# Loads, sums and stores of the output weights' blocks pinned to their written place

## The chip, the cores and the metric

The kernel runs on one core of one Trainium2 chip. The metric is the time of one execution in microseconds of the device (us). Below, PE is TensorE (matmuls), DVE is VectorE, ACT is ScalarE, POOL is GpSimd, and SP is SyncE, which here only issues DMAs; DMA is the set of 16 transfer engines that carry them out.

## The reference

One layer of a transformer trunk in float32 (sequence 1024, width 1024, 16 heads): a forgetting-attention mixer, then a SwiGLU channel mixer of width 2816, each between a modulation and a LayerNorm. The change lies in the channel mixer:

```
def swiglu(h, w_in, w_out):
    gate, up = jnp.split(h @ w_in, 2, axis=-1)
    return (jax.nn.silu(gate) * up) @ w_out

x = layer_norm(DEEPNORM_ALPHA * x + gate1 * y, ln_g[i, 0], ln_b[i, 0])
h = x * (1.0 + scale2) + shift2
x = layer_norm(DEEPNORM_ALPHA * x + gate2 * swiglu(h, ffn_w_in[i], ffn_w_out[i]), ln_g[i, 1], ln_b[i, 1])
```

## The kernel before

Every float32 product is made of three matmuls of a high and a low part (hi x hi, hi x lo, lo x hi). The kernel works in three long stages: attention (to about 720 us), the first product of the channel mixer ("first product", to about 1210 us) and the second product with the output weights ("second product", to the end). Both products of the channel mixer use a scheme with seven sub-products instead of eight (a Strassen form), so sums and differences of blocks are needed on both sides.

**First product.** `seq` is a list of 154 steps `(ff, i)`: ff is one of 22 column tiles of 128 hidden units, i the sub-product. The steps of ff 0 to 5 with i = 1 and 2 come first; then each ff from 0 to 5 has five steps (6, 7, 5, 4, 3), and from ff 6 on, at n = 42, each ff has seven (1, 6, 2, 7, 5, 4, 3). `step(n)` issues 12 matmuls of 512 columns (lines 1072 to 1074) into one of the banks A, B and D, and then what reads the bank: for i = 6, 7 and 4 DVE reads B (lines 1085, 1087, 1092), for i = 5 and 3 it reads D (lines 1089, 1096), for i = 1 and 2 ACT reads A (lines 1081, 1083). B and D have one buffer each, and a chain goes on adding in the same bank, so the matmuls of i = 7 have to wait until DVE has read the bank of i = 6, those of i = 4 until that of i = 7 is read, and those of i = 3 until that of i = 5. In the same step `prepare(n + 8)` splits the weights for a later step into high and low part: a cast on ACT (line 844) and a subtraction on DVE (line 845), which one of eight slots takes. ff and ff + 1 also share sums of hidden values (`hidden_sums`, lines 990 to 995, on DVE) that wait for POOL's products (line 1098) and are stored to DRAM (line 981, `sd`).

**The blocks of the output weights.** The second product needs differences of blocks of `ffn_w_out`. `out_weights(j, k)` makes them, for j = 0 to 10, in two 512 KB buffers that are free by then, `gate1b` and `gate2b`: at k = 0 it loads two blocks (line 1006, two DMAs of 512 KB on SP), at k = 7 DVE makes two differences (lines 1008 and 1009), at k = 8 two more (lines 1011 and 1012), and both buffers are stored to `td[j]` (line 1014, two DMAs of 512 KB). There is one set of buffers, so block j + 1 can be loaded when block j is stored. In the source `step(n)` calls it with

```
j, k = divmod(n - 7 * FIRST, 10)
if 0 <= j < NJ:
    out_weights(j, k)
```

so a block is written over ten steps: load at n = 42 + 10 j, differences seven and eight steps later, and the last store at n = 150 of 154.

**What sets the order.** Each engine runs its instructions in the order of its own list, and SP issues its DMAs likewise: an instruction that waits holds up all that stand behind it. The written order is not the order in the lists: before the program is built, a scheduler puts each engine's instructions in order by a simulation of its own of when each is ready, keeping only true dependences. `tc.keep_in_program_order(ins)` takes an instruction out of that freedom: it ties it behind the instruction that was written before it on the same engine. It adds no wait on another engine.

**Second product.** `prep2(m)` takes raw blocks `r` (a half from `sd`, a half from `ffn_w_out` or `td`, lines 870 to 875), casts them on ACT (line 1028) and subtracts on DVE (line 1029) into a ring of 14 places. `products` (lines 1221 to 1223) uses them. `done` (line 1180) copies the first sub-product's banks on ACT; the four banks lie in pairs in two tiles, y1_0 and y1_1.

Of the kernel before, what the change touches and what calls it, by code (L numbers as in the profile page):

```python
# [12 lines left out]
ALU = mybir.AluOpType  # L13
# [3 lines left out]
P = 128  # L17
# [28 lines left out]
def fox_trunk_kernel(  # L46
# [17 lines left out]
    nc = tc.nc  # L64
# [5 lines left out]
    fwo = ffn_w_out[0]  # L70
# [788 lines left out]
    td = [dram.tile([P, 2, 2, 512], F32, name=f"td{j}") for j in range(NJ)]  # L859
# [113 lines left out]
        return others  # L973

    banks, fds = {}, []

    def open_bank(tag, ff, n):
        banks[tag, ff] = psA.tile([P, 512], F32, name=f"{tag}{ff}", tag=tag, bufs=n)
# [21 lines left out]
    def out_weights(j, k):  # L1000

        b11, b12 = gate1b[:, 0:512], gate1b[:, 512:1024]
        b21, b22 = gate2b[:, 0:512], gate2b[:, 512:1024]
        if k == 0:
            for n, t in enumerate((gate1b, gate2b)):
                nc.sync.dma_start(t, fwo[(2 * j + n) * P:(2 * j + n + 1) * P, :])
        elif k == 7:
            nc.vector.tensor_tensor(b11, b12, b11, ALU.subtract)
            nc.vector.tensor_tensor(b12, b22, b12, ALU.subtract)
        elif k == 8:  # L1010
            nc.vector.tensor_tensor(b22, b22, b11, ALU.subtract)
            nc.vector.tensor_tensor(b21, b21, b22, ALU.subtract)
            for n, t in enumerate((gate1b, gate2b)):
                nc.sync.dma_start(td[j][:, n].rearrange("p c e -> p (c e)"), t)


    RING = 14
# [39 lines left out]
    def step(n):  # L1057
# [9 lines left out]
        if 0 <= j < NJ:  # L1067
            out_weights(j, k)
# [234 lines left out]
```

## Time and profile before

| what | value |
|---|---|
| median of 3 runs | 1439.01 us (1437.71 to 1443.9) |
| the profiled execution's own time | 1438.14 us |
| its span, first to last instruction | 1436.3 us |
| mean granted TensorE clock | 0.990 of full speed |
| PE busy | 1359.0 us, 95% |
| DVE, ACT, POOL busy | 1012.2, 584.2, 334.4 us |
| DMA moved | 254.41 MB, mean 177 GB/s |

The page gives busy time by engine over the whole span, and the span in 40 slices of 35.9 us. Busy shares are averages over stages with different limits: what a change in one stage is worth is read from that stage, in the tables by stretch, in the waits of PE there, and in the lists of instructions in order of time. In those lists the square bracket at a row's end is the engine's idle time before the instruction, and what ended it.

### The profile page before, as it was taken

What the parts mean: (1) busy time and instruction counts of PE and PEld (TensorE: products, weight loads), DVE (VectorE), ACT (ScalarE), POOL (GpSimd) and SP (SyncE); (2) the same over time, 40 slices, a digit from 0 to 9 for tenths busy, and PEclk for the clock granted to TensorE, in tenths of its full rate; (3) what the DMA queues carried; (4) which work ended last, traced back from release to release, by engine and by line L of the source; (5) the groups of instructions that cost most, each with busy time, mean ns of one, the idle gap of its engine ahead of it and who ended that gap; (6) DMA issues with size and microseconds to landing.
All of it is one profiled execution on the core that took longest, in us unless ns stands there. A gap on an engine that the chain in (4) does not pass through costs nothing.

```text
span 1436.3 us, 19137 instructions
## 1 busy us (share of the span) xinstructions
PE 1359.0 (95%) x6832; PEld 1134.0 (79%) x6832; DVE 1012.2 (70%) x1636; ACT 584.2 (41%) x1025; POOL 334.4 (23%) x250
## 2 busy tenths in 40 slices
PE   5899999999999999999999888999999999899997
PEld 4677778877888888879998667777788888788886
DVE  6866586555888888888778555767655556775897
ACT  3532232224777777774338222222223334533320
POOL 2442012210111111141000544434444431000011
PEclk9999999999999999999999999999999999999999
DMA  9757775558555555627463234777732336976531
GB/s 275 197 176 243 240 218 177 183 194 212 143 135 137 132 139 136 148 87 266 162 193 93 89 110 132 259 243 261 248 111 96 110 111 208 352 256 225 195 119 73
DMA packets 212305, 254.41 MB, mean 177 GB/s; under 512 B 13353, under 2 KB 138609, under 8 KB 212210
## 3 DMA queue, kind: packets, MB, share of 16 engines
q1 hardware_dynamic: 211058, 251.09, 57.9%
q10 hardware_dynamic: 1152, 2.10, 0.4%
q8 instruction: 54, 0.88, 0.3%
q14 instruction: 41, 0.34, 0.1%
HBM read 185.18 MB, written 67.96 MB: 176 GB/s over the span
## 4 chain that ended last, share of the span: by engine, by line
PE 63%; DVE 14%; DMA 9%; POOL 6%; issue 4%; ACT 2%; SPq 1%; POOLq 0%; DVEq 0%; ACTq 0%
PE og L631 5%; PE t L596 4%; PE y L1221 4%; PE y L1223 4%; PE y L1222 4%; PE B L1072 3%; PE B L1073 3%; PE B L1074 3%; PE s L535 2%; PE A L1072 2%; PE A L1074 2%; PE A L1073 2%; PE s L536 2%; PE o L579 2%; PE D L1074 2%
## 5 line engine op out<-in xcount | busy, mean ns | idle before, releaser
L1221 PE MATMUL y<-ring 128*128 128x512 f32 (+1 forms) x319 | 122.8, 385 | 4.7 <-ACT fpu L1180 4.3
L1072 PE MATMUL B<-XT,slots 128*128 128x512 f32 x264 | 106.9, 405 | 19.7 <-DVE fd L1085 16.7
L1029 DVE TENSOR_TENSOR ring<-r,ring 128x1024 fp32r<-128x1024 f32 x77 | 95.6, 1249 | 41.3 <-ACT ring L1028 36.2
L1028 ACT CAST ring<-r 128x1024 fp32r<-128x1024 f32 x77 | 80.5, 1053 | 107.7 <-PE y L1223 57.5
L1222 PE MATMUL y<-ring 128*128 128x512 f32 (+1 forms) x319 | 122.7, 385 | 0.0
L1223 PE MATMUL y<-ring 128*128 128x512 f32 (+1 forms) x319 | 122.4, 385 | 0.0
L602 DVE TENSOR_TENSOR pl<-t,ph 128x512 fp32r<-128x512 f32 x192 | 103.9, 549 | 14.8 <-ACT ph L601 13.4
L844 ACT CAST slots<-wi 128x512 fp32r<-128x512 f32 x88 | 54.2, 621 | 143.9 <-PE D L1073 73.0
L543 ACT ACTIVATE p<-s,nm 128x640 f32<-128x640 f32 (+7 forms) x128 | 95.5, 746 | 39.1 <-DVE nm L542 38.7
L601 ACT CAST ph<-t 128x512 fp32r<-128x512 f32 x192 | 90.9, 479 | 44.2 <-PE t L596 41.8
L1073 PE MATMUL B<-XT,slots 128*128 128x512 f32 x264 | 105.2, 399 | 0.0
L1074 PE MATMUL B<-XT,slots 128*128 128x512 f32 x264 | 105.0, 398 | 0.0
L542 DVE TENSOR_REDUCE nm<-s 128x1 f32<-128x640 f32 (+7 forms) x128 | 95.6, 748 | 2.5
L596 PE MATMUL t<-ident,p 128*128 128x128 f32 x576 | 95.7, 274 | 0.6 <-DVE pl L602 0.5
L596 PEld LDWEIGHTS t<-ident,p 128*128 128x128 f32 x576 | 71.3, 141 | 11.5 <-DVE pl L602 2.2
L1072 PEld LDWEIGHTS B<-XT,slots 128*128 128x128 f32 x264 | 50.9, 193 | 36.1 <-DVE fd L1085 21.8
L579 PE MATMUL o<-ph,va 128*128 128x512 f32 x192 | 76.6, 399 | 0.0
L845 DVE TENSOR_TENSOR slots<-wi,slots 128x512 fp32r<-128x512 f32 x88 | 71.0, 807 | 7.7 <-ACT slots L844 7.7
L1221 PEld LDWEIGHTS y<-ring 128*128 128x128 f32 x319 | 60.3, 189 | 18.1 <-ACT fpu L1180 4.7
L535 PE MATMUL s<-ka,qa 128*128 128x320 f32 (+2 forms) x192 | 67.5, 352 | 4.8 <-ACT p L543 4.8
L1223 PEld LDWEIGHTS y<-ring 128*128 128x128 f32 x319 | 60.4, 189 | 11.8
L1072 PE MATMUL A<-h2h,slots 128*128 128x512 f32 x176 | 69.2, 393 | 0.6 <-ACT fc L1081 0.6
(571 smaller groups left out, 3731.8 us busy)
## 6 DMA issues: line engine op xcount, KB each, us to landing
wi<-in_ffn_w_in_dram SPq DMA_DIRECT2D x50, 512.0 KB
aw<-in_ada_w_dram SPq DMA_DIRECT2D x46, 512.0 KB
r<-sd SPq DMA_DIRECT2D x77, 256.0 KB
sd<-hs SPq DMA_DIRECT2D x44, 256.0 KB
r<-td SPq DMA_DIRECT2D x44, 256.0 KB
sd<-fd SPq DMA_DIRECT2D x33, 256.0 KB
r<-in_ffn_w_out_dram SPq DMA_DIRECT2D x33, 256.0 KB
qa<-qs SPq DMA_DIRECT2D x32, 256.0 KB
```

The lines of the kernel that those rows point to most:

```text
L535: nc.tensor.matmul(o, qa[:, q], ka[:, c0:c0 + w], start=True, stop=False)
L542: nc.vector.tensor_reduce(nm, view, axis=axis, op=ALU.max, negate=True)
L579: nc.tensor.matmul(o[:, c0:], va[:, kbk, :], ph[:, c0:], start=(kbk == 0), stop=False)
L596: nc.tensor.transpose(tb[:, jj * P:(jj + 1) * P], probs[hf * 4 + jj][:, kbk * P:(kbk + 1) * P], ident)
L602: nc.vector.tensor_tensor(pl[:, c0:], tb[:, c0:], f32(ph[:, c0:]), ALU.subtract)
L1029: nc.vector.tensor_tensor(t[:, 1], raw, f32(t[:, 0]), ALU.subtract)
L1072: nc.tensor.matmul(b, hi, rh, start=(first and k == 0), stop=False, skip_group_check=True)
L1073: nc.tensor.matmul(b, hi, rl, start=False, stop=False, skip_group_check=True)
L1074: nc.tensor.matmul(b, lo, rh, start=False, stop=(k == 3), skip_group_check=True)
L1221: nc.tensor.matmul(b[:, c0:c1], sh, wh, start=first, stop=False, skip_group_check=True)
L1222: nc.tensor.matmul(b[:, c0:c1], sh, wl, start=False, stop=False, skip_group_check=True)
L1223: nc.tensor.matmul(b[:, c0:c1], sl, wh, start=False, stop=last, skip_group_check=True)
```

## The change

Each instruction that `out_weights` issues (per block two loads, four differences on DVE and two stores) is passed to `keep_in_program_order`. Nothing else is edited. One line is added above them, so a line number above 976 is one higher in the changed kernel.

```
     banks, fds = {}, []
+    keep = tc.keep_in_program_order
...
         if k == 0:
             for n, t in enumerate((gate1b, gate2b)):
-                nc.sync.dma_start(t, fwo[(2 * j + n) * P:(2 * j + n + 1) * P, :])
+                keep(nc.sync.dma_start(t, fwo[(2 * j + n) * P:(2 * j + n + 1) * P, :]))
         elif k == 7:
-            nc.vector.tensor_tensor(b11, b12, b11, ALU.subtract)
-            nc.vector.tensor_tensor(b12, b22, b12, ALU.subtract)
+            keep(nc.vector.tensor_tensor(b11, b12, b11, ALU.subtract))
+            keep(nc.vector.tensor_tensor(b12, b22, b12, ALU.subtract))
         elif k == 8:
-            nc.vector.tensor_tensor(b22, b22, b11, ALU.subtract)
-            nc.vector.tensor_tensor(b21, b21, b22, ALU.subtract)
+            keep(nc.vector.tensor_tensor(b22, b22, b11, ALU.subtract))
+            keep(nc.vector.tensor_tensor(b21, b21, b22, ALU.subtract))
             for n, t in enumerate((gate1b, gate2b)):
-                nc.sync.dma_start(td[j][:, n].rearrange("p c e -> p (c e)"), t)
+                keep(nc.sync.dma_start(td[j][:, n].rearrange("p c e -> p (c e)"), t))
```

The order of instructions differs in three places that the prediction speaks of. The first is DVE's list where ff 6 ends and ff 7 begins. B and D are the banks (B6 is B of ff 6), `slots` the split weights, `fd` the hidden values, `hs` their sums. Before:

```order
L1087 TENSOR_TENSOR fd_8631<-B6_9209,fc_8277 128x512
L845 TENSOR_TENSOR slots_7830<-sqb_8409,slots_7830 128x512
L1008 TENSOR_TENSOR gate1b_106<-gate1b_106 128x512
L1089 TENSOR_TENSOR fd_8631<-D6_9268,fd_8631 128x512
L845 TENSOR_TENSOR slots_7830<-wi71_22_9042,slots_7830 128x512
L1009 TENSOR_TENSOR gate1b_106<-gate2b_107,gate1b_106 128x512
L1011 TENSOR_TENSOR gate2b_107<-gate2b_107,gate1b_106 128x512
L1092 TENSOR_TENSOR fd_8631<-B6_9209,fc_8277 128x512
L845 TENSOR_TENSOR slots_7830<-skb_8410,slots_7830 128x512
L1012 TENSOR_TENSOR gate2b_107<-gate2b_107 128x512
L1096 TENSOR_TENSOR fd_8631<-D6_9268,fd_8631 128x512
```

With the change, from the subtraction after L1089 (now L1090) to the first reading of B7:

```order
L845 TENSOR_TENSOR slots_7830<-wi71_22_9042,slots_7830 128x512
L1093 TENSOR_TENSOR fd_8631<-B6_9209,fc_8277 128x512
L845 TENSOR_TENSOR slots_7830<-skb_8410,slots_7830 128x512
L1097 TENSOR_TENSOR fd_8631<-D6_9268,fd_8631 128x512
L845 TENSOR_TENSOR slots_7830<-wi80_23_9165,slots_7830 128x512
L1009 TENSOR_TENSOR gate1b_106<-gate1b_106 128x512
L995 TENSOR_TENSOR hs3_7_9501<-fd_8631 128x512
L1010 TENSOR_TENSOR gate1b_106<-gate2b_107,gate1b_106 128x512
L845 TENSOR_TENSOR slots_7830<-wi81_24_9167,slots_7830 128x512
L1012 TENSOR_TENSOR gate2b_107<-gate2b_107,gate1b_106 128x512
L1013 TENSOR_TENSOR gate2b_107<-gate2b_107 128x512
L1086 TENSOR_TENSOR fd_8631<-B7_9344,fc_8277 128x512
```

Before, this is already block 1 of the output weights, and block 2 begins three rows later; with the change it is block 0, and the four differences of block 1 come ten steps later. In the list of before the eleven blocks stand between the first reading of B5 and the second of B12; with the change they are spread from here to the readings of ff 21.

The second place is SP's list of DMAs in the same part of the program. `wi` are weights of the first product, `sd` stores of hidden values, `td` the stores of a block, `gate1b` and `gate2b` its loads. Before:

```order
L1006 DMA gate1b<-in_ffn_w_out_dram 128x1024
L1006 DMA gate2b<-in_ffn_w_out_dram 128x1024
L804 DMA wi_26_9302<-in_ffn_w_in_dram 128x8x128
L1014 DMA td_7052<-gate1b 128x1024
L981 DMA sd_3_6977<-fd 128x512
L1014 DMA td_7052<-gate2b 128x1024
L1006 DMA gate1b<-in_ffn_w_out_dram 128x1024
L981 DMA sd_3_7043<-hs_7_9501 128x512
L1006 DMA gate2b<-in_ffn_w_out_dram 128x1024
L804 DMA wi_27_9428<-in_ffn_w_in_dram 128x8x128
```

With the change:

```order
L1007 DMA gate1b<-in_ffn_w_out_dram 128x1024
L804 DMA wi_27_9428<-in_ffn_w_in_dram 128x8x128
L1007 DMA gate2b<-in_ffn_w_out_dram 128x1024
L804 DMA wi_28_9430<-in_ffn_w_in_dram 128x8x128
L982 DMA sd_3_6988<-fd 128x512
L982 DMA sd_3_7010<-fd 128x512
L982 DMA sd_3_7021<-hs_7_9499 128x512
L982 DMA sd_3_7032<-hs_7_9500 128x512
L982 DMA sd_3_6999<-hs_7_9502 128x512
L804 DMA wi_29_9567<-in_ffn_w_in_dram 128x8x128
L1015 DMA td_7052<-gate1b 128x1024
L1015 DMA td_7052<-gate2b 128x1024
```

Between the loads of a block and its stores there were one or two other DMAs, now there are about eight. The two stores of the last block, which stood between `wi_37` and `wi_38`, now stand among the loads `r` of the second product, behind `r_7` and ahead of half of `r_8`; the broadcast load of `gate2b` for the end (line 1236), which must follow them, moved with them to a place between `r_13` and `r_14`.

The third place is ACT's list where the first sub-product of the second product ends: the casts of ring places and the copies of its banks. Before:

```order
L1028 CAST ring3_11317<-r2_20_11481 128x1024
L1028 CAST ring3_11317<-r2_21_11555 128x1024
L1028 CAST ring4_11374<-r2_22_11560 128x1024
L1180 COPY fpu_11351<-y1_0_11360 128x512
L1180 COPY fpu_11351<-y1_1_11361 128x512
L1028 CAST ring4_11374<-r2_23_11578 128x1024
```

With the change:

```order
L1029 CAST ring3_11317<-r2_20_11481 128x1024
L1181 COPY fpu_11351<-y1_0_11360 128x512
L1181 COPY fpu_11351<-y1_1_11361 128x512
L1181 COPY fpu_11351<-y1_0_11360 128x512
L1029 CAST ring3_11317<-r2_21_11555 128x1024
L1181 COPY fpu_11351<-y1_1_11361 128x512
```

Three copies moved ahead of the casts of `r2_21` and `r2_22`. On POOL nothing moves, and on PE some three or four matmuls at two places.

## Rows read from the trace of the kernel before

**Rows 1.** Table by stretch, all engines: busy us (instructions), granted clock, DMA share, GB/s.
```profile
core 0: us, PE busy (x) PEld busy (x) DVE busy (x) ACT busy (x) POOL busy (x), PEclk, DMA share, GB/s
877.00:1034.00 157.00, 146.37 (x625) 117.29 (x625) 108.65 (x150) 43.65 (x75) 62.60 (x44) 0.99 0.71 241
1034.00:1190.00 156.00, 156.00 (x690) 129.20 (x689) 80.17 (x117) 48.92 (x82) 66.31 (x47) 1.00 0.34 114
1190.00:1250.00 60.00, 55.68 (x238) 45.44 (x237) 42.60 (x40) 31.86 (x35) 6.58 (x4) 0.97 0.83 280
935.00:965.00 30.00, 26.43 (x108) 20.74 (x107) 19.99 (x29) 8.11 (x14) 9.89 (x8) 0.94 0.68 237
```
**Rows 2.** Waits of PE, 877 to 1034 us: total us, times, longest.
```profile
PE D L1072 <- DVE fd L1089: 5.5, 3, 2.3
PE B L1072 <- DVE fd L1085: 4.5, 6, 1.3
```
**Rows 3.** DVE in order of time, four readings of bank B: start, duration.
```profile
869.99 0.69 DVE L1087 TENSOR_TENSOR fd<-B,gate1b 128x512 f32<-128x512 f32 x1 [2.29 <-PE B L1074]
...
1036.87 0.69 DVE L1092 TENSOR_TENSOR fd<-B,fc 128x512 f32<-128x512 f32 x1 [0.62 <-PE B L1074]
...
1164.71 0.69 DVE L1087 TENSOR_TENSOR fd<-B,fc 128x512 f32<-128x512 f32 x1 [1.54 <-PE B L1074]
...
1183.75 0.69 DVE L1087 TENSOR_TENSOR fd<-B,fc 128x512 f32<-128x512 f32 x1 [1.54 <-PE B L1074]
```
**Rows 4.** Groups by line, the differences on DVE, 877 to 1034 us.
```profile
L1008 DVE TENSOR_TENSOR gate1b<-gate1b 128x512 f32<-128x512 f32 x11 | 11.7, 1061 | 13.2 <-DMA gate1b<-in_ffn_w_out_dram 13.2
L1012 DVE TENSOR_TENSOR gate2b<-gate2b 128x512 f32<-128x512 f32 x11 | 9.8, 887 | 0.2
L1009 DVE TENSOR_TENSOR gate1b<-gate2b,gate1b 128x512 f32<-128x512 f32 x11 | 8.8, 797 | 12.0 <-DMA gate2b<-in_ffn_w_out_dram 11.8
L1011 DVE TENSOR_TENSOR gate2b<-gate2b,gate1b 128x512 f32<-128x512 f32 x11 | 8.5, 775 | 0.2
```
**Rows 5.** SP in order of time: a load of a block's second half.
```profile
944.15 0.84 SPq L1006 DMA_DIRECT2D gate2b<-in_ffn_w_out_dram  x1
```
**Rows 6.** DVE in order of time behind that load.
```profile
950.70 0.93 DVE L1009 TENSOR_TENSOR gate1b<-gate2b,gate1b 128x512 f32<-128x512 f32 x1 [2.36 <-DMA gate2b<-in_ffn_w_out_dram]
...
953.22 0.68 DVE L1089 TENSOR_TENSOR fd<-D,fd 128x512 f32<-128x512 f32 x1
```
**Rows 7.** PE in order of time, two of its stalls.
```profile
953.95 0.50 PE L1072 MATMUL D<-XB,slots 128*128 128x512 f32 x1 [2.34 <-DVE fd L1089]
...
986.64 0.50 PE L1072 MATMUL B<-XT,slots 128*128 128x512 f32 x1 [0.89 <-DVE fd L1085]
```
**Rows 8.** DVE in order of time ahead of the second of these stalls.
```profile
978.31 1.78 DVE L1012 TENSOR_TENSOR gate2b<-gate2b 128x512 f32<-128x512 f32 x1
980.01 0.68 DVE L1096 TENSOR_TENSOR fd<-D,fd 128x512 f32<-128x512 f32 x1
...
985.30 0.69 DVE L1008 TENSOR_TENSOR gate1b<-gate1b 128x512 f32<-128x512 f32 x1
985.90 0.69 DVE L1085 TENSOR_TENSOR fd<-B,fc 128x512 f32<-128x512 f32 x1
```
**Rows 9.** DVE in order of time, ff 21: ring places ahead of a bank.
```profile
1198.44 3.72 DVE L1029 TENSOR_TENSOR ring<-r,ring 128x1024 fp32r<-128x1024 f32 x3 [0.34 <-ACT ring L1028]
...
1204.64 0.69 DVE L1087 TENSOR_TENSOR fd<-B,fc 128x512 f32<-128x512 f32 x1
```
**Rows 10.** ACT in order of time, the end of the first sub-product of the second product.
```profile
1238.73 1.05 ACT L1028 CAST ring<-r 128x1024 fp32r<-128x1024 f32 x1 [0.33 <-DMA r<-td]
...
1243.59 1.07 ACT L1180 COPY fpu<-y 128x512 f32<-128x512 f32 x2
```
**Rows 11.** PE in order of time, the matmul that follows that copy.
```profile
1244.22 0.56 PE L1221 MATMUL y<-ring 128*128 128x512 f32 x1 [4.32 <-ACT fpu L1180]
```

## The prediction

> **What bounds the kernel now.** I read first the table by stretch [rows 1]. The page says PE is busy for 95% of the span, but that is a mean over stages. From 1034 to 1190 us PE is busy for 156.00 of 156 us: nothing there waits that costs time. From 877 to 1034 us it is busy for 146.37 of 157 us, although the steps (ff, i) are of the same kind. What differs is what runs beside PE: DMA share 0.71 against 0.34, DVE busy 108.65 against 80.17 us. That is the stretch into which the eleven blocks of the output weights are pressed, one in 14 us or so, where the source has one in ten steps.
>
> Second, PE's waits there [rows 2]: nearly all are for DVE's reading of a bank (lines 1089 and 1085). Third, what DVE did before such a reading. The groups of the four differences [rows 4] show DVE idle ahead of them for 13.2 + 12.0 us, waiting for the blocks' loads. One case in full: the second load of a block is issued at 944.15 [rows 5], the difference that needs it waits 2.36 us for it and starts at 950.70, and the reading of bank D, which stands behind it in DVE's list, starts at 953.22 [rows 6]; PE waits 2.34 us for it [rows 7]. So the path there is load, difference, bank, PE, and only because the difference stands too early in DVE's list.
>
> **What a step costs, and what the stretch loses.** From the DVE reading at 1164.71 to the same reading of the next ff at 1183.75 [rows 3] are seven steps: 19.04 / 7 = 2.72 us a step. From the reading after i = 7 of ff 4 at 869.99 to that after i = 4 of ff 12 at 1036.87 (both waited for PE, so they show where PE was) are 3 + 5 + 42 + 6 = 56 steps: 56 x 2.72 = 152.3 us, but 166.9 us went by. **The stretch loses 14.6 us.** Of these 157 - 146.4 = 10.6 us are PE's idle time [rows 1]. The granted clock is 0.94 of full speed from 935 to 965 us [rows 1], where PE has just stood still for 2.34 us [rows 7]; it has two levels, 2.4 GHz and half of that, so this is about 0.06 x 30 = 1.8 us of work. The last 2.2 us lie in the starts after ten stalls.
>
> **The change part by part.** It adds no instruction, removes none and adds no wait; it moves the blocks' instructions.
>
> *Loads and differences.* A load is now issued up to seven steps, 19 us, ahead of the difference that needs it. Seen from issue to use it takes 950.70 - 944.15 = 6.6 us [rows 5, 6] while DMA is 0.71 busy. With the same traffic over some 290 us, DMA should be 0.34 + 0.37 x 157 / 290 = 0.54 busy, so even a load that SP issues ten us late is there in time. The 25.2 us in which DVE waited for loads should go to about zero. Gain: the 14.6 us, at most. At least nothing, if the loss is due to DVE's work and not to its waits (a rival, below). I take nearly all, because 25.2 us of waits stand ahead of readings that PE lost 10.6 us for.
>
> *The work that stays.* Each block still costs DVE 1.06 + 0.80 + 0.78 + 0.89 = 3.5 us [rows 4]. With all eleven in the stretch after 877 us, DVE is 69% busy without its waits; spread, it is some 51% + 3.5 / 27.2 = 64%. In the new list I laid each block between the readings, with 0.6 us from one difference to the next (985.30 to 985.90 [rows 8]). A bank's reading has one step, 2.72 us, before PE needs it, less its own 0.7: 2.0 us of slack. The four differences fall between readings with room in most blocks; in five of them the reading of line 1085 is 0.3 to 0.9 us late, within the slack. What can go over it is a difference that POOL slows, to 1.78 us instead of 0.69 [rows 8]. One stall of before shows this without a load's wait at its place: 978.31 slow, the chain over ACT and POOL to the sums is late, the reading is at 985.90, PE waits 0.89 us [rows 7, 8]. Bounds: no such stall, or one in each block, 11 x 0.89 = 9.8 us. I take 1.5 us, near the lower end, since from 1034 us on the same POOL work runs beside DVE and PE never waits.
>
> *The last block.* It now lies in ff 21, where DVE also fills the ring. Before, the reading of line 1087 starts at 1204.64 right behind five ring subtractions [rows 9], with PE about to need it. Three differences are put ahead of it: 3 x 0.6 = 1.8 us, of which 0.34 us fits where DVE waited for ACT. Four matmuls of the second product were moved ahead of PE's wait (0.9 us). Left: 0 to 1.5 us; I take 0.5 us.
>
> *The start of the second product.* PE waits 4.32 us for a copy on ACT [rows 11] that starts at 1243.59, behind two casts which wait for loads [rows 10]. Now the copy stands right behind the cast of `r2_20`, which started at 1238.73: it could start at 1239.7, 3.9 us earlier. Against this, two stores and one load of 0.5 MB each move into this stretch, where DMA is 0.83 busy at 280 GB/s [rows 1]: 1.5 MB there are 5.6 us if all of it delays `r2_20`, and nothing if it fits in the gaps. So the copy moves by -3.9 to +1.7 us, and if the stall gets short the clock's fall after it (0.97 over 60 us [rows 1], 1.8 us) goes too. Bounds -5.7 to +1.7; I take -1.
>
> *SP's queue.* The stores wait for the differences and hold up the weights `wi` behind them. Before, they did so too, and PE's waits [rows 2] name no load of weights. Nothing.
>
> **Sum.** -14.6 + 1.5 + 0.5 - 1 = -13.6 us against the profiled execution: 1438.1 - 13.6 = 1424.5 us. The median of the runs shown is 0.9 us above that execution; I forecast **1425 us**. About 0.5%, 7 us, is what a measurement of this kernel can tell from no change.
>
> **Rivals.**
>
> *It is DVE's work, not its waits.* The differences are as many as before; if each block still brings a stall like that at 986.64, 9.8 us come back: 1425 + 8 = 1433 us. For it: that stall, and DVE's stretched differences. Against it: DVE's waits for loads are 25.2 us, its stretching is only 11 x (3.5 - 2.8) = 8 us, and the three longest stalls of PE [rows 2] follow line 1089. Chance 0.14.
>
> *Blocks beside POOL's work make every block stall: slower.* In the new places the four differences may all meet a POOL instruction. If each takes the 1.78 us of the slow one [rows 8] where it now fills 0.6, the readings behind come 4.7 us late, 2.7 us over the slack; with a fall of the clock (1.8 us) that is 4.5 us a block, 50 us for eleven, and 1438 - 15 + 50 = 1473 us. The turning point is 14.6 / 11 = 1.3 us lost in each block. The means [rows 4] speak against it: 0.2 to 0.4 us over 0.69, not 1.1. The Trainium skill speaks for it (SBUF — State Buffer, "Who interferes with whom"): a DVE instruction with both inputs in SBUF is locked out for a whole POOL instruction that reads SBUF, and the four differences are of that kind; the slow row agrees in kind. Chance 0.05.
>
> *The head of the second product gives it back.* The last stores wait for DVE in SP's list, ahead of half of `r_8` and of `r_9` and `r_12`; if these and the 1.5 MB delay the ring by the full 5.6 us and the stall at 1244 grows by 1.7 us and a second one opens, some 7 us return: 1432 us. Against it: PE uses a ring place in 2.72 us and is many places behind the casts at 1238. Chance 0.08.
>
> *The order does not change what runs.* Excluded for the lists: they differ as shown. That the loss was there for another reason (DMA contention as such) would leave 1438 us; the stretch after 1034 us can't decide it. Chance 0.03.
>
> **How the numbers follow.** The forecast, 1419 to 1430 us, has 0.70. Its low end takes the bound -5.7 us at the copy and the whole 14.6 us: 1439 - 20.3 = 1419; its high end three more us of late readings and the copy at +1.7. The range reaches to the first and third rival: **1418 to 1435 us**; beyond it lie the slower rival, no change, and the worst of the first. Faster by over 0.5% (under 1431.8 us): 0.70 and about half of the two rivals at 1432 and 1433, 0.81. Within 0.5%: 0.14. Slower: 0.05.
>
> **What the changed profile would show.** Right: the rows of the differences with no DMA wait ahead of them, DMA share near 0.54 from 900 to 1190 us, PE busy for over 98% there, and ff after ff 19.0 to 19.4 us apart. ff 12's reading comes near 1022 instead of 1036.87. The copy's stall is under 4.5 us. Wrong would be: PE waits for lines 1086, 1088 or 1090 that add up to over 5 us after 900 us (work, not waits), or a new wait of PE on ring places after 1200 us.

## The result, and the profile after

The changed kernel takes **1422.17 us** (median of 4 runs, 1420.45 to 1424.15); the kernel before took 1438.36 us in the runs beside it. The ratio is 0.988, with a 95% interval of 0.9851 to 0.9909: faster by 1.2%. Two more sets of runs of the same kernel, on two other occasions, gave 0.9912 (0.9888 to 0.9935) and 0.9888 (0.9864 to 0.9911). The profiled execution takes 1424.15 us (span 1422.4), 14.0 us less than that of before. I had forecast 1425 us, 1418 to 1435.

First the table by stretch of the changed kernel (columns as in [rows 1]).

```profile
core 0: us, PE busy (x) PEld busy (x) DVE busy (x) ACT busy (x) POOL busy (x), PEclk, DMA share, GB/s
877.00:1034.00 157.00, 156.47 (x691) 129.25 (x690) 98.01 (x137) 49.26 (x83) 71.53 (x50) 1.00 0.53 176
1034.00:1190.00 156.00, 156.00 (x690) 129.18 (x689) 98.57 (x136) 51.71 (x83) 64.76 (x44) 1.00 0.55 183
1190.00:1250.00 60.00, 54.84 (x235) 44.70 (x234) 45.25 (x42) 29.35 (x31) 3.68 (x2) 0.94 0.93 323
```

Against [rows 1], the two stretches now look alike: DMA share 0.53 and 0.55 (0.71 and 0.34 before), DVE busy 98 us in both (109 and 80 before), and PE busy for 156.47 us of 157 where it had 146.37. PE's waits for DVE, which were 5.5 and 4.5 us [rows 2], are one of 0.5 us from 877 to 1190 us, at 882 us, behind a sum of hidden values and ahead of the first block's differences:

```profile
PE B L1073 <- DVE fd L1086: 0.5, 1, 0.5
```

The four differences, by line, in the changed kernel from 877 to 1200 us (columns as in [rows 4]). The idle time for DMA, 13.2 and 12.0 us there, is gone; the work itself is no shorter, 3.8 us a block where it was 3.5.

```profile
L1009 DVE TENSOR_TENSOR gate1b<-gate1b 128x512 f32<-128x512 f32 x11 | 10.8, 984 | 0.0
L1013 DVE TENSOR_TENSOR gate2b<-gate2b 128x512 f32<-128x512 f32 x11 | 10.5, 956 | 0.3
L1010 DVE TENSOR_TENSOR gate1b<-gate2b,gate1b 128x512 f32<-128x512 f32 x11 | 10.5, 954 | 0.2
L1012 DVE TENSOR_TENSOR gate2b<-gate2b,gate1b 128x512 f32<-128x512 f32 x11 | 9.7, 883 | 0.0
```

One block in full, in order of time: SP's load of the first half, then DVE 21 us later.

```profile
918.16 0.33 SPq L1007 DMA_DIRECT2D gate1b<-in_ffn_w_out_dram  x1
```
```profile
939.31 0.69 DVE L1009 TENSOR_TENSOR gate1b<-gate1b 128x512 f32<-128x512 f32 x1
940.03 1.66 DVE L1010 TENSOR_TENSOR gate1b<-gate2b,gate1b 128x512 f32<-128x512 f32 x1
941.61 0.68 DVE L1088 TENSOR_TENSOR fd<-B,fc 128x512 f32<-128x512 f32 x1
...
943.53 1.67 DVE L1013 TENSOR_TENSOR gate2b<-gate2b 128x512 f32<-128x512 f32 x1
945.12 0.68 DVE L1090 TENSOR_TENSOR fd<-D,fd 128x512 f32<-128x512 f32 x1
```

Two differences ran 1.7 us instead of 0.7, the readings of L1088 and L1090 start right behind them, and PE does not stop: a late reading has its two us of slack.

Where the time came from is seen at one reading in each ff, that of line 1093 (1092 before). In order of time, of the changed kernel, ff 5 and ff 12, and then the same of ff 5 in the kernel before (its ff 12 stands in [rows 3]):

```profile
889.25 0.69 DVE L1093 TENSOR_TENSOR fd<-B,gate2b 128x512 f32<-128x512 f32 x1 [1.32 <-PE B L1075]
...
1019.81 0.69 DVE L1090 TENSOR_TENSOR fd<-D,fd 128x512 f32<-128x512 f32 x1 [1.43 <-PE D L1075]
...
1024.02 0.68 DVE L1093 TENSOR_TENSOR fd<-B,fc 128x512 f32<-128x512 f32 x1
```
```profile
889.57 0.69 DVE L1092 TENSOR_TENSOR fd<-B,gate2b 128x512 f32<-128x512 f32 x1 [0.67 <-PE B L1074]
```

From ff 5 to ff 12 went 1036.87 - 889.57 = 147.3 us before and 1024.02 - 889.25 = 134.8 us now. The reading at 1024.02 is itself some 1.5 us late (no PE wait stands at it; the last one that waited for PE is 1019.81, and one step of 2.72 us later is 1022.5). The same measure splits every run below; the table is worked out from that reading in each profile, ff 0, 5, 12 and 21, and the span's end.

| profiled execution of | ff 0 to 5 | 5 to 12 | 12 to 21 | 21 to the end |
|---|---|---|---|---|
| before | 87.8 | 147.3 | 174.1 | 225.4 |
| changed | 83.7 | 134.8 | 173.4 | 225.0 |
| changed, second and third set | 84.0, 87.1 | 134.8, 134.8 | 172.8, 173.7 | 225.4, 224.9 |

The change shows in the second column alone, by 12.5 us. The first column varies by 3 us between executions of one kernel, so single spans that differ by 3 us say nothing.

Not every microsecond of it stood behind a load. Of PE's ten stalls from 877 to 1034 us in the kernel before (10.6 us), four, 6.5 us together, wait for a reading that has a wait for a load close ahead of it in DVE's list, as in [rows 6, 7]. Three (2.0 us) wait for a reading that has ahead of it both a wait for a load and a sum of hidden values that waits for POOL. Three (2.1 us) have no wait for a load close ahead: two of them, that of [rows 8] included, come behind such a sum, and the third is for a reading by ACT.

### The profile page after: what moved, and what is told of

The parts are those of the page before. It is cut to its first block, busy times and chain, and to the rows that moved or that the text cites. A ratio compares the mean times of both kernels' runs of the same rounds, so it can differ in the third digit from the quotient of the medians.

```text
span 1422.4 us, 19155 instructions
## 1 busy us (share of the span) xinstructions
PE 1354.8 (95%) x6832; PEld 1134.3 (80%) x6832; DVE 1011.5 (71%) x1636; ACT 585.2 (41%) x1025; POOL 340.1 (24%) x250
## 4 chain that ended last, share of the span: by engine, by line
PE 70%; DVE 12%; DMA 5%; POOL 5%; issue 4%; ACT 2%; SPq 1%; POOLq 0%; DVEq 0%; ACTq 0%
PE og L631 5%; PE y L1222 4%; PE y L1223 4%; PE y L1224 4%; PE B L1073 4%; PE t L596 4%; PE B L1075 4%; PE B L1074 4%; PE A L1073 3%; PE A L1074 3%; PE A L1075 3%; PE D L1075 3%; PE D L1074 2%; PE D L1073 2%; PE s L535 2%
## 5 line engine op out<-in xcount | busy, mean ns | idle before, releaser
L1073 PE MATMUL B<-XT,slots 128*128 128x512 f32 x264 | 105.0, 398 | 15.7 <-DVE fd L1086 12.7
L1074 PE MATMUL B<-XT,slots 128*128 128x512 f32 x264 | 103.7, 393 | 0.0
L1075 PE MATMUL B<-XT,slots 128*128 128x512 f32 x264 | 103.7, 393 | 0.0
L1222 PEld LDWEIGHTS y<-ring 128*128 128x128 f32 x319 | 60.3, 189 | 18.5 <-ACT fpu L1181 5.6
L1224 PEld LDWEIGHTS y<-ring 128*128 128x128 f32 x319 | 60.4, 189 | 11.8
L1223 PEld LDWEIGHTS y<-ring 128*128 128x128 f32 x319 | 60.4, 189 | 11.6
```

Source lines behind the costliest of these rows:

```text
L1073: nc.tensor.matmul(b, hi, rh, start=(first and k == 0), stop=False, skip_group_check=True)
L1074: nc.tensor.matmul(b, hi, rl, start=False, stop=False, skip_group_check=True)
L1075: nc.tensor.matmul(b, lo, rh, start=False, stop=(k == 3), skip_group_check=True)
L1222: nc.tensor.matmul(b[:, c0:c1], sh, wh, start=first, stop=False, skip_group_check=True)
L1223: nc.tensor.matmul(b[:, c0:c1], sh, wl, start=False, stop=False, skip_group_check=True)
L1224: nc.tensor.matmul(b[:, c0:c1], sl, wh, start=False, stop=last, skip_group_check=True)
```

## Experiments

Theory W: DVE met loads that were still under way, with a bank's reading next in its list. Theory P: the blocks were pressed together, and it is the DMA traffic or DVE's work in 157 us that cost. All are edits of the changed kernel, and ratios are to the kernel before.

### Pressed, but with loads in time

```
-        elif k == 7:
+        elif k == 3:
...
-        elif k == 8:
+        elif k == 4:
...
-        j, k = divmod(n - 7 * FIRST, 10)
+        j, k = divmod(n - 7 * FIRST, 5)
```

> The changed kernel with a block every five steps (13.6 us, as closely as in the kernel before) and the differences three and four steps behind the loads, pinned. DMA share from 877 to 1034 us should be near 0.7 and DVE's busy share near 0.69 again, but a load leads its use by 8.2 us. Theory W (waits for loads): as fast as the changed kernel within 4 us, 1418 to 1426 us, hardly a DMA wait ahead of the differences and under 2 us of PE stalls in the stretch. Theory P (the pressing itself, by DVE work or by DMA contention): the stretch loses 8 to 15 us again, 1430 to 1438 us.

Measured: 1424.39 us, ratio 0.9911 (0.9881 to 0.9941); the four runs take 1419.78 to 1426.73 us, and the profile is of the fastest. Table by stretch, one group of differences, and all waits of PE from 877 to 1190 us:

```profile
877.00:1034.00 157.00, 156.82 (x692) 129.26 (x691) 113.97 (x156) 48.72 (x82) 74.83 (x50) 1.00 0.71 241
```
```profile
L1010 DVE TENSOR_TENSOR gate1b<-gate2b,gate1b 128x512 f32<-128x512 f32 x11 | 9.6, 868 | 4.7 <-DMA gate2b<-in_ffn_w_out_dram 4.5
```
```profile
PE D L1073 <- DVE fd L1090: 0.2, 1, 0.2
```

This speaks against theory P. The DMA share (0.71, 241 GB/s) is to the digit that of [rows 1], DVE is busier (114 against 109 us), and PE loses nothing: ff 5 to 12 takes 134.0 us. With the loads in time, neither this traffic nor this work costs PE anything.

### Pressed, and with loads too late

```
-        elif k == 7:
+        elif k == 1:
...
-        elif k == 8:
+        elif k == 2:
...
+        elif k == 4:
             for n, t in enumerate((gate1b, gate2b)):
...
-        j, k = divmod(n - 7 * FIRST, 10)
+        j, k = divmod(n - 7 * FIRST, 5)
```

> A block every five steps as in the run with pressed blocks (DMA share 0.7), but the differences one and two steps behind the loads and the stores kept at k = 4, so that the next loads have to follow late stores and the differences come upon loads that are still under way: a lead of some 3 us where a load needs 4 to 6. Theory W (DVE waits for loads ahead of a bank's reading): DMA waits of 1 to 3 us ahead of the differences in most blocks, 15 to 40 us in all, and PE stalls of 0.5 to 2 us a block, 6 to 20 us in all between 880 and 1040 us; 1428 to 1445 us. Theory P (the pressing or the place in the list, not the waits): as the pressed run with the longer lead, a ratio of 0.991, 1418 to 1426 us.

Measured: 1431.35 us (8 runs), ratio 0.9958 (0.9938 to 0.9978), against 1423.51 us for the changed kernel beside it. The waits are back, though fewer than expected; groups of the differences, then the longest case on DVE, then PE.

```profile
L1009 DVE TENSOR_TENSOR gate1b<-gate1b 128x512 f32<-128x512 f32 x11 | 13.5, 1229 | 6.4 <-DMA gate1b<-in_ffn_w_out_dram 6.3
...
L1010 DVE TENSOR_TENSOR gate1b<-gate2b,gate1b 128x512 f32<-128x512 f32 x11 | 9.5, 867 | 3.4 <-DMA gate2b<-in_ffn_w_out_dram 3.2
```
```profile
998.73 0.69 DVE L1009 TENSOR_TENSOR gate1b<-gate1b 128x512 f32<-128x512 f32 x1 [4.08 <-DMA gate1b<-in_ffn_w_out_dram]
999.34 0.68 DVE L1087 TENSOR_TENSOR fd<-B,fc 128x512 f32<-128x512 f32 x1
```
```profile
1000.08 0.50 PE L1074 MATMUL B<-XT,slots 128*128 128x512 f32 x1 [1.36 <-DVE fd L1087]
```

A wait of 4.08 us gives a stall of 1.36 us: load, difference, bank, PE, as in [rows 5 to 7]. With 9.5 us of DMA waits, ff 5 to 12 takes 138.7 us, 3.9 us more than in the changed kernel. In the profiled execution another 3 us lie in ff 0 to 5 (87.1 us), which the edit does not touch and which varies; what else the 7.8 us between the medians hold is not shown. Of PE's five stalls from 877 to 1190 us (3.75 us) two, of 1.36 and 1.43 us, stand behind waits for loads. So W holds in kind. The two pressed runs differ in the lead of the loads, in the place of the stores and in the steps at which the differences stand; that such a place costs nothing by itself is seen in the next run, which has the differences at the same k. W's low ends were too high (9.5 us of waits where 15, and 3.75 us of stalls where 6 were expected), and only a third of the 12.5 us came back there.

### Spread, with the differences close behind the loads

```
-        elif k == 7:
+        elif k == 1:
...
-        elif k == 8:
+        elif k == 2:
```

> The changed kernel, spread over the same ten steps a block and pinned, but the differences are written one and two steps behind the loads (k = 1, 2) instead of seven and eight. Work, traffic and spread stay; only the lead of the loads shrinks from some 19 us to 2.7 to 5.4 us, where a load took 6.6 us from issue to use. Theory W (the stretch lost time because DVE waited for loads ahead of a bank's reading): DVE rows of the first two differences show idle time for DMA again, 2 to 4 us a block, PE waits for the readings return between 880 and 1190 us, 0.5 to 1.5 us in each of eleven blocks, so 1427 to 1437 us. Theory P (the loss came from pressing the blocks' work and traffic together): no change against the changed kernel, 1420 to 1424 us, and no stall of PE there.

Measured: 1423.7 us, ratio 0.9909 (0.9886 to 0.9932). W's forecast of 1427 us and more missed, because its premise did: the written distance in steps is not the lead in time. SP runs ahead of the steps, and a block's load went out well before, as one pair shows (SP, then DVE):

```profile
912.70 0.38 SPq L1007 DMA_DIRECT2D gate1b<-in_ffn_w_out_dram  x1
```
```profile
L1009 DVE TENSOR_TENSOR gate1b<-gate1b 128x512 f32<-128x512 f32 x11 | 10.5, 958 | 1.9 <-DMA gate1b<-in_ffn_w_out_dram 1.9
```

The difference for that load started at 924.63. In all eleven blocks the lead of the first load was 4.9 to 16 us, and 1.9 us of waits in all is too little to tell the theories apart. PE has no stall behind a block.

### One half of the pins at a time

Only the differences pinned (loads and stores float):

```
-                keep(nc.sync.dma_start(t, fwo[(2 * j + n) * P:(2 * j + n + 1) * P, :]))
+                nc.sync.dma_start(t, fwo[(2 * j + n) * P:(2 * j + n + 1) * P, :])
...
-                keep(nc.sync.dma_start(td[j][:, n].rearrange("p c e -> p (c e)"), t))
+                nc.sync.dma_start(td[j][:, n].rearrange("p c e -> p (c e)"), t)
```

> Only the four differences on DVE are pinned; loads and stores float in the scheduler's order again. Theory W: the differences stand where they stand in the changed kernel, far behind their loads, so the time is that of the changed kernel within 3 us, no DMA wait ahead of the differences, no PE stall between 882 and 1190 us. Rival (the place of the loads and stores on the SP queue carries part of the gain): 1427 to 1437 us, with DMA waits ahead of the differences or of weights wi.

Measured: 1420.17 us, ratio 0.9889 (0.9863 to 0.9915); ff 5 to 12 takes 134.8 us, and no difference waits for DMA. SP, in order of time, block 1: within 0.01 us of where the pinned one stood.

```profile
918.17 0.33 SPq L1007 DMA_DIRECT2D gate1b<-in_ffn_w_out_dram  x1
```

The pins on SP's DMAs add nothing: a block cannot be loaded before the block ahead of it has been stored, and that cannot happen before its differences. Pinned differences hold the DMAs in place, but for the first block's load, which has no block ahead of it and went out 11 us earlier.

Only the loads and stores pinned (the differences float):

```
-            keep(nc.vector.tensor_tensor(b11, b12, b11, ALU.subtract))
+            nc.vector.tensor_tensor(b11, b12, b11, ALU.subtract)
...
```

> The other half alone: loads and stores are pinned, the four differences float. In the scheduler's list they now stand a step or two earlier than written, some four to six steps behind their loads, since the pinned loads spread the blocks as well. Theory W (only a difference that comes upon a load still under way costs time): no DMA wait ahead of the differences, no PE stall between 882 and 1190 us beyond 1 us in all, the time of the changed kernel within 3 us. Rival (only a place pinned on DVE gives the gain): 1427 to 1438 us with stalls in the stretch again.

Measured: 1425.99 us, ratio 0.9917 (0.989 to 0.9943), 3.6 us above the changed kernel beside it. The text's premise was wrong: the differences did not stand four to six steps behind the loads but came 3.5 to 7 us behind them, and waited in every block.

```profile
L1009 DVE TENSOR_TENSOR gate1b<-gate1b 128x512 f32<-128x512 f32 x11 | 10.4, 950 | 9.4 <-DMA gate1b<-in_ffn_w_out_dram 9.4
L1010 DVE TENSOR_TENSOR gate1b<-gate2b,gate1b 128x512 f32<-128x512 f32 x11 | 8.4, 759 | 9.2 <-DMA gate2b<-in_ffn_w_out_dram 9.2
```
```profile
993.69 0.69 DVE L1009 TENSOR_TENSOR gate1b<-gate1b 128x512 f32<-128x512 f32 x1 [1.13 <-DMA gate1b<-in_ffn_w_out_dram]
995.91 0.69 DVE L1010 TENSOR_TENSOR gate1b<-gate2b,gate1b 128x512 f32<-128x512 f32 x1 [1.53 <-DMA gate2b<-in_ffn_w_out_dram]
...
997.84 1.66 DVE L1013 TENSOR_TENSOR gate2b<-gate2b 128x512 f32<-128x512 f32 x1
999.43 0.68 DVE L1088 TENSOR_TENSOR fd<-B,fc 128x512 f32<-128x512 f32 x1
```
```profile
1000.16 0.50 PE L1073 MATMUL B<-XT,slots 128*128 128x512 f32 x1 [0.82 <-DVE fd L1088]
```

Here is the price list that the argument needed. Waits of 18.6 us in 20 pieces of 0.3 to 1.5 us (one of 3.06) cost some 3.4 us (ff 5 to 21: 311.9 against 308.5 us in the changed kernel beside it), while before 25.2 us, in pieces up to 3.4 us, stood in a stretch that lost 12.5. By these stalls what counts is not the sum of the waits but what each has over the slack of two us, together with what stands behind it, a slowed difference here. Spreading alone, with waits left in every block, brought most of the gain.

### Twice the work on DVE

```
+        elif k == 4:
+            keep(nc.vector.tensor_tensor(b11, b12, b11, ALU.subtract))
+            keep(nc.vector.tensor_tensor(b12, b22, b12, ALU.subtract))
+        elif k == 6:
+            keep(nc.vector.tensor_tensor(b12, b22, b12, ALU.subtract))
+            keep(nc.vector.tensor_tensor(b11, b12, b11, ALU.subtract))
```

> The changed kernel with twice the work for the blocks on DVE: at k = 4 the first two differences are made and at k = 6 taken back (the output is the same up to rounding), so 44 more differences of 0.9 us, 41 us, none of which waits for anything; DVE's busy share between 877 and 1190 us goes from 0.63 to about 0.76. If work as such does not count as long as a reading has its two us of slack: PE stalls in the stretch below 3 us, the ratio of the changed kernel plus at most 0.002. Rival (it is DVE's work and not its waits): the extra work costs what the blocks' own work was said to cost, 5 to 13 us, 1428 to 1436 us, with stalls of PE behind lines 1086 to 1094.

Measured: 1426.78 us, ratio 0.9925 (0.9898 to 0.9951), against 1422.35 us and 0.9888 beside it: +4.4 us, above the +0.002 of my theory and just under the rival's range. The intervals overlap, so the trace has to speak.

```profile
877.00:1190.00 313.00, 309.30 (x1356) 253.53 (x1355) 235.37 (x313) 97.24 (x161) 140.12 (x92) 1.00 0.53 177
```
```profile
970.52 0.69 DVE L991 TENSOR_TENSOR hs<-fd 128x512 f32<-128x512 f32 x1 [1.19 <-POOL fd L1105]
971.13 0.69 DVE L1019 TENSOR_TENSOR gate2b<-gate2b 128x512 f32<-128x512 f32 x1
...
973.54 0.68 DVE L1092 TENSOR_TENSOR fd<-B,fc 128x512 f32<-128x512 f32 x1
```
```profile
974.27 0.50 PE L1079 MATMUL B<-XT,slots 128*128 128x512 f32 x1 [1.42 <-DVE fd L1092]
```

DVE is 75% busy there (235.37 of 313 us), and PE has two new stalls, of 1.42 and 1.43 us, each where a block meets sums that wait for POOL; ff 5 to 12 and 12 to 21 grow by 2.9 and 2.5 us. So 47 us more of work cost some 5 us: work is not free, it is cheap, and in the changed kernel (63% busy) it costs nothing yet.

### The head of the second product

A block every eight steps, so that the last one is out of the way early:

```
-        elif k == 7:
+        elif k == 6:
...
-        elif k == 8:
+        elif k == 7:
...
-        j, k = divmod(n - 7 * FIRST, 10)
+        j, k = divmod(n - 7 * FIRST, 8)
```

> The changed kernel with a block every eight steps, differences at k = 6 and 7: the last block ends in ff 17 or 18, its two stores and the broadcast load of the last row's weights lie ahead of the second product's loads, and the copies at the end of the first sub-product stand on ACT where they stood in the kernel before. Theory T (the changed kernel loses 2 to 3 us at the head of the second product because the last block's traffic and the moved SP rows are in its way): PE's stall behind the copy falls from 5.2 us to under 4.3, 1417 to 1420 us. If the tail's placement does not matter: 1421 to 1424 us and a stall of about 5 us.

Measured: 1424.1 us, ratio 0.9916 (0.9891 to 0.9941), a stall of 4.47 us: no gain (the other two executions of the changed kernel have stalls of 4.47 and 4.92 us, so 4.47 is no fall). The trace shows why. ACT in order of time: the casts of `r2_20`, `r2_21` and `r2_22` and the copy behind them.

```profile
1222.46 1.05 ACT L1029 CAST ring<-r 128x1024 fp32r<-128x1024 f32 x1 [0.35 <-DMA r<-td]
1225.01 1.04 ACT L1029 CAST ring<-r 128x1024 fp32r<-128x1024 f32 x1 [1.50 <-DMA r<-td]
1226.36 1.05 ACT L1029 CAST ring<-r 128x1024 fp32r<-128x1024 f32 x1 [0.30 <-DMA r<-td]
1227.31 1.07 ACT L1181 COPY fpu<-y 128x512 f32<-128x512 f32 x2
```

The same place in the changed kernel, where the copy stands behind `r2_20`, and PE's wait for it:

```profile
1229.09 1.05 ACT L1029 CAST ring<-r 128x1024 fp32r<-128x1024 f32 x1 [0.34 <-DMA r<-td]
1230.04 1.07 ACT L1181 COPY fpu<-y 128x512 f32<-128x512 f32 x2
```
```profile
1230.67 0.80 PE L1222 MATMUL y<-ring 128*128 128x512 f32 x1 [5.16 <-ACT fpu L1181]
```

From the reading of line 1093 in ff 21 (1210.93 before, 1197.45 changed, 1193.95 here) to the cast of `r2_20` it is 27.8 us before, 31.6 us in the changed kernel, 28.5 us here: the last block in its late place, with its 1.5 MB and its rows in SP's list, does delay `r2_20` by some 3 us, as feared; which of the two does it is not shown. To the copy it is 32.7, 32.6 and 33.4 us: what the order gives in the changed kernel the late block takes, and without the late block the old order is back, with `r2_21` and `r2_22` ahead of the copy.

The copy can be taken out of PE's way instead:

```
-                    if j == NJ - 1:
+                    if j == NJ - 1 and i != 1:
+                        done(i, r, bs[r])
+                if j == NJ - 1 and i == 1:
+                    for r in range(4):
                         done(i, r, bs[r])
```

> The changed kernel, where the four copies of the first sub-product's banks are issued behind its last matmul instead of one by one between them. PE then does not meet a copy in a pair of banks that it is still adding to. Theory: the stall of 5.2 us at 1230 us and the half clock of 6.8 us behind it go, so 5 to 8 us less than the changed kernel: 1414 to 1418 us. Rival: the ring places are the true limit there (casts behind loads), the stall moves to a ring place one or two matmul groups later and the time stays at 1420 to 1424 us.

Measured: 1417.11 us, ratio 0.9861 (0.9836 to 0.9887). Table by stretch:

```profile
1190.00:1250.00 60.00, 60.00 (x266) 49.67 (x265) 45.84 (x41) 32.90 (x35) 3.68 (x2) 1.00 0.91 320
```

PE never stops there, the granted clock is 1.00 where it was 0.94, and ff 21 to the end takes 218.6 us where the three executions of the changed kernel take 224.9 to 225.4. The ratio's interval still touches that of the changed kernel. The ring was not the limit.

### The same mechanism, another wait

In ff 1 to 4 the scheduler puts a sum that waits for POOL ahead of a reading, as it did with the differences, four times in all. In the changed kernel, DVE and then PE:

```profile
847.11 1.73 DVE L995 TENSOR_TENSOR hs<-fd 128x512 f32<-128x512 f32 x1 [2.63 <-POOL fd L1099]
848.77 0.68 DVE L1086 TENSOR_TENSOR fd<-B,fc 128x512 f32<-128x512 f32 x1
```
```profile
849.50 0.50 PE L1073 MATMUL B<-XT,slots 128*128 128x512 f32 x1 [2.73 <-DVE fd L1086]
```

```
     def hidden_sums(ff, k, ua, ub, va, vb):
+        kept = keep if ff < FIRST else (lambda x: x)
...
-            nc.vector.tensor_tensor(hs[1], ub, vb, ALU.add)
+            kept(nc.vector.tensor_tensor(hs[1], ub, vb, ALU.add))
...
```

(and so for the other three sums, on top of the moved copies)

> The kernel with the copies moved, and in it the four sums of hidden values of ff 1, 3 and 5 (lines 991 to 996 in the changed kernel) pinned to their written place as the change does it for the blocks: in the changed kernel one of them stands ahead of a reading of bank B and waits 2.6 us for POOL, five times, and PE stalls 12.2 us for it between 790 and 870 us. If what counts is a waiting instruction ahead of a reading, whoever it waits for, these stalls go, and with them the clock's fall (0.95 over 67 us): 9 to 15 us less than the kernel with the copies moved, a ratio of 0.976 to 0.980 to the kernel before, some 1402 to 1408 us. Rival: the pinned sums stand one or two rows later, ahead of the next reading of B, and make that one late: 3 to 12 us of stalls stay, now for line 1088, and the ratio is 0.980 to 0.987.

Measured: **1403.54 us, ratio 0.9774 (0.9751 to 0.9797)**, the fastest of all, 2.3% under the kernel before. PE's waits from 780 to 1260 us, and the table by stretch:

```profile
PE B L1073 <- DVE fd L1088: 4.5, 3, 3.1
PE B L1073 <- DVE fd L1086: 1.2, 1, 1.2
```
```profile
780.00:877.00 97.00, 91.30 (x388) 72.95 (x387) 62.18 (x84) 27.75 (x46) 52.55 (x36) 0.98 0.38 117
```

In the changed kernel PE waited 12.2 us for line 1086 up to 877 us. Four of these five waits, 2.73 us each, were behind such a sum, not five as expected, and they are gone; the fifth, of 1.24 us, has no sum ahead of it and stays. So does the wait of 3.1 us for line 1088, which was 3.0 us in the changed kernel. ff 0 to 5 now takes 71.0 us instead of 83.7. Some of the rival came true: 0.53 and 0.88 us of new stalls for line 1088, each behind two sums of 1.78 and 1.67 us. The first pair:

```profile
821.58 1.78 DVE L991 TENSOR_TENSOR hs<-fd 128x512 f32<-128x512 f32 x1
823.40 1.67 DVE L992 TENSOR_TENSOR hs<-hs,fd 128x512 f32<-128x512 f32 x1
```

The changed kernel itself was run twice more, as a measure beside these runs.

> The changed kernel itself once more, as the measure for the runs beside it on this chip: a ratio of 0.985 to 0.991 to the kernel before.

> The changed kernel itself, as the measure for the two runs beside it: a ratio of 0.987 to 0.993 to the kernel before.

Measured: 1423.51 us, ratio 0.9912 (0.9888 to 0.9935), and 1422.35 us, ratio 0.9888 (0.9864 to 0.9911).

## Why the prediction was right

The profiled execution came out at 1424.15 us where the sum gave 1424.5. The term that decides, the stretch, was right in mechanism and size. That the sum met the time to 0.4 us is luck in part: two terms taken 2.0 us too high and one taken 1.8 us too low nearly cancel. Term by term:

- **The stretch, -14.6 us.** Between the reading after i = 7 of ff 4 (869.99 before; 870.53 in the changed kernel) and the reading of ff 12 (1022.5 without its own lateness) lie 152.0 us instead of 166.9: -14.9. The mechanism is shown: the pressed run with loads in time keeps the gain, the pressed run with late loads gives 3.9 us of it back, with stalls behind the waits. That late loads account for the whole 14.9 us is not shown: 2.1 us of the stalls had no load's wait close ahead of them.
- **Loads and differences.** The waits went from 25.2 us to zero, and the lead is 17 to 24 us in all blocks. But the step that took waits as the measure ("25.2 us of waits stand ahead of readings that PE lost 10.6 us for") was loose: 18.6 us of short waits cost 3.4 us. One reading was wrong too: of the three longest stalls only two (2.34 and 1.92 us) follow line 1089, the third (1.29 us) follows line 1085. The size came out because I took it from PE's side, by steps of 2.72 us.
- **The work that stays, +1.5 us.** Measured 0: eleven of the 44 differences were slowed, and no reading was over the slack. Doubled work costs 5 us, so the bound was right to be there.
- **The last block, +0.5 us.** Measured 0. One difference stands ahead of the reading of ff 21, which starts at 1191.16, and PE does not wait.
- **The start of the second product, -1 us.** This is the term that was wrong in sign, within its bounds. The copy moved by -0.1 us against ff 21's reading, not by -3.9: the order's gain of 3.9 us, which I had as one end, came in full, and against it `r2_20` came 3.8 us later, where the other end had 5.6. PE arrived 0.9 us earlier, so the stall grew from 4.32 [rows 11] to 5.16 us (4.47 and 4.92 in the other two executions), where a stall under 4.5 us had been named as a sign of being right.
- **SP's queue, 0.** So it was: no wait of PE for weights.

Sum as measured: -14.9 + 0 + 0 + 0.8 = -14.1 us, against 14.0 us between the two executions. Of the signs, DMA share (0.54 from 900 to 1190 us) and PE busy (all of that stretch) came as named. Of the rivals, "DVE's work, not its waits" fell with the pressed run, and with it "DMA contention as such"; "the head gives it back" was right in kind (the late block delays `r2_20`) and 0.8 us in size. The slower rival had its collisions and not its price, as the last section tells.

## What to carry to other kernels

Where an engine's list is set by a scheduler, look for instructions with a long idle time that stand ahead of the one instruction which the bound engine needs, whatever they wait for; pin those; here their DMAs needed no pin, since they followed by dependence. Judge a wait by what it has over the slack of the reading behind it, not by the sum of the waits, and measure the loss at the bound engine's own milestones. A written distance in steps is no lead in time: read issue and use from the trace.

## What had not been expected of the hardware

The slowed differences have one pattern. In the changed kernel eleven of the 44 take 1.66 to 1.78 us, and each of them starts while a POOL instruction is under way and ends some 0.55 us after it; POOL, in order of time, beside the block shown above (939.31 to 945.12):

```profile
939.47 1.67 POOL L829 TENSOR_TENSOR sqb<-wi,wi 128x512 f32<-128x512 f32 x1 [6.69 <-DVE slots L845]
942.97 1.68 POOL L828 TENSOR_TENSOR sqb<-wi 128x512 f32<-128x512 f32 x1 [1.83 <-DVE slots L845]
```

939.47 + 1.67 = 941.14, and the difference begun at 940.03 ends at 941.69. One that began before POOL did (939.31) runs its 0.69 us undisturbed. The Trainium skill states such a lockout for DVE instructions with two inputs in SBUF beside POOL instructions that read SBUF (SBUF — State Buffer, "Who interferes with whom"). The trace agrees, with 1.0 us as the cost of a collision. Since one in four differences collides in the changed kernel, and there never two ahead of one reading, the slack took all of them. Two collisions ahead of one reading do go over it: in the run with pinned sums the two sums shown there end at 823.36 and 825.07, 0.55 us behind two POOL instructions (822.81 and 824.51), and PE waits 0.53 us; the other such pair costs it 0.88 us.

The other surprise is the clock in ff 0 to 5: with the same stalls of 2.73 us in every execution, that stretch takes 84 us in some and 87 in others of the same kernel, and without the stalls the granted clock there is 0.98 instead of 0.91 to 0.96 from 780 to 877 us. What decides how long it stays at the lower level was not tried.
